# Hybrid decoder block, one core: the adaLN shift and later terms as VectorE dot products, the first scale on TensorE in pairs of tiles

## The chip, the core and the metric

One Trainium2 chip, one of its cores. TensorE multiplies matrices, VectorE and ScalarE work element by element on 128 partitions, GpSimd does little here, and DMA queues bring the weights from HBM. The metric is the device time of one launch in microseconds (us); the kernel before takes 1477.01 us, median of 3 runs (1475.06 to 1477.59).

## The reference

A decoder block on 256 tokens of width 2048, all in float32:

```
c_act = silu(c)
mod = c_act @ w_ada + b_ada                    # 2048 x 12288
sh1, sc1, gt1, sh2, sc2, gt2 = split(mod, 6)
h = rms_norm(x, g_pre_mix) * (1 + sc1) + sh1
z = h @ w_in                                   # 2048 x 8000
mix = (gate_a * mla(z) + gate_b * swa(z)) @ w_o
x = x + gt1 * rms_norm(mix, g_post_mix)
h = rms_norm(x, g_pre_ffn) * (1 + sc2) + sh2
u = causal_dwconv(h @ w_up)                    # 2048 x 11264
x = x + gt2 * rms_norm((silu(u1) * u2) @ w_down, g_post_ffn)
```

`mod` is a product of one row vector with a matrix of 100 MB: each of its weights is read once from HBM and used once. It makes 192 tiles of 128x1024 float32 (512 KB each), 32 for each of the six terms.

## The kernel before, in words

**Products.** Every large product is done three times over in a reduced float format: a weight tile `raw` is split into `whi` (ScalarE, L115) and `wlo` = raw - whi (VectorE, L116), the activations likewise (`split_pair`, L157 and L158), and TensorE adds hi·hi, hi·lo and lo·hi (`mm3`, L128 to L130, and its variants at L135 to L145).

**Order of work.** x comes in transposed (`xT`: channels on partitions). `early_z` multiplies h with half of `w_in` in six groups of k-tiles of 128 channels (`KGS` = 2, 2, 2, 2, 4, 4), called z0 to z5 below. While TensorE does group kg, a generator `early_gen` computes scale and shift of group kg + 1, scales xT with rstd, then with s1 and sh1 (L281, VectorE), and splits it to h. It is advanced by `pump`, once at each weight tile, at a rate. After the six groups come the attention (`step`, `late_z`, `pair_proj`), w_o, the passage to the second norm, w_up and w_down. The later four terms (gt1, s2, sh2, gt2) are generators `cols_gen`, pumped in z5, through the attention, w_o and w_up. The instructions of each engine are put in order ahead of time by a scheduler that simulates the engines; each engine then runs its own list in that order.

**How adaLN is computed.** `ada_gen` loads a tile of 1024 weights a partition (the contracted channels on partitions). On TensorE (L233) silu(c) is the stationary operand, as one column of a block of 32 (`cpad`), and the tile's columns are cut in four parts that go to the four groups of 32 columns of the array. On VectorE (L239, L241) the tile is multiplied with its silu(c) and added to `acc`; at the end four matmuls with `ones` (L246) add up the partitions. Either way the result lies in four rows, is copied to `rows` (L248) and turned into columns by matmuls with the identity (L269, L299). `SHARE` gives all tiles of groups 1 to 3 to TensorE, and every second tile of the last three to VectorE. The later terms are on VectorE alone.

**Buffers.** In the early groups adaLN tiles have four buffers of their own (`raw2`), w_in tiles five (`raw`); later all share the five. All loads are issued by one queue (SP, L94 and L101), in order.

Of the kernel before, what the change touches and what calls it, by code (L numbers as in the profile page):

```python
# [42 lines left out]
def block_kernel(ctx: ExitStack, tc: tile.TileContext, a, out: bass.AP):  # L43
    nc = tc.nc
    pe, act, dve, pool = nc.tensor, nc.scalar, nc.vector, nc.gpsimd
    PS = bass.MemoryType.PSUM
# [128 lines left out]
    xT = xp.tile([P, KC, T], F32, name="xT")  # L175
# [4 lines left out]
    ones = const.tile([P, P], F32, name="ones")  # L180
    pool.memset(ones, 1.0)
# [26 lines left out]
    for k in range(0, KC, 2):
        sq = xp.tile([P, 512], F32, tag="sq", bufs=2, name="sq").rearrange("p (a b) -> p a b", a=2)
        act.activation(sq, xT[:, k:k + 2, :], AF.Square)  # L210
        for i in range(2):
            pe.matmul(ps_ss[:, :T], ones, sq[:, i, :], start=(k + i == 0), stop=(k + i == KC - 1))
# [5 lines left out]
    def ada_gen(src, width, rows, col, on_pe, share=10**9, spread=False):  # L218


        nj = KC // src.shape[0]
        w = 4 * width
        n = src.shape[0]
        acc = None
        ps = bank(on_pe) if on_pe else None
        for t in range(n):
            raw = load_bg(src[t], nj * w, spread and t % 2 == 1)
            for i in range(nj):
                j = t * nj + i
                if on_pe and t % share != share - 1:  # L230
                    for g in range(4):
                        o = i * w + g * width
                        pe.matmul(ps[32 * g:32 * g + 32, :width], cpad[:, j, :], raw[:, o:o + width],  # L233
                                  start=(j == 0), stop=(j == KC - 1 and share > n))
                    continue
                r = raw[:, i * w:i * w + w]
                if acc is None:
                    acc = const.tile([P, WT], F32, tag="acc", bufs=1, name="acc")
                    dve.tensor_scalar(acc[:, :w], r, csil[:, j:j + 1], None, op0=ALU.mult)  # L239
                else:  # L240
                    dve.scalar_tensor_tensor(acc[:, :w], r, csil[:, j:j + 1], acc[:, :w], op0=ALU.mult, op1=ALU.add)  # L241
            yield
        if acc is not None:
            ps = ps if on_pe else bank("tp")
            for g in range(4):
                pe.matmul(ps[32 * g:32 * g + 32, :width], ones[:, :32], acc[:, g * width:g * width + width],  # L246
                          start=not on_pe, stop=True)
        act.copy(rows[:, col:col + width], ps[:, :width])  # L248

    rows = const.tile([P, 512], F32, name="rows")  # L250
# [4 lines left out]

    def early_gen(kg, k0, s):

        w = s * 64
# [9 lines left out]
        for b in range(nb):
            pe.matmul(ps[:, 4 * b:4 * b + 4], rows[:, b * P:(b + 1) * P], ident[:, 0:P:32], start=True, stop=True)  # L269

        pv = ps[:, :4 * nb].rearrange("p (b g) -> p g b", g=4)
        bs = bada[:, KC + k0:KC + k0 + s].rearrange("p (g b) -> p g b", g=2)
        s1v = s1[:, k0:k0 + s].rearrange("p (g b) -> p g b", g=2)
        dve.scalar_tensor_tensor(s1v, pv[:, 0:2, :], 1.0, bs, op0=ALU.add, op1=ALU.add)
        dve.tensor_tensor(s1[:, k0:k0 + s], s1[:, k0:k0 + s], gcol[:, G_MIX + k0:G_MIX + k0 + s], op=ALU.mult)
        dve.tensor_tensor(sh1[:, k0:k0 + s].rearrange("p (g b) -> p g b", g=2), pv[:, 2:4, :],
                          bada[:, k0:k0 + s].rearrange("p (g b) -> p g b", g=2), op=ALU.add)
# [11 lines left out]

    def cols_gen(which, dst, bofs, gofs):  # L290

        for half in range(2):
            yield from ada_gen(a["w_ada2"][which][half], T, rows, half * T, None)

        for _ in range(4 if which == 3 else 0):
            yield
        ps = bank("tp")
        for b in range(4):
            pe.matmul(ps[:, 4 * b:4 * b + 4], rows[:, b * P:(b + 1) * P], ident[:, 0:P:32], start=True, stop=True)  # L299

        dve.tensor_tensor(dst.rearrange("p (g b) -> p g b", b=4), ps[:, 0:16].rearrange("p (b g) -> p g b", g=4),
                          bada[:, bofs:bofs + KC].rearrange("p (g b) -> p g b", b=4), op=ALU.add)
# [212 lines left out]
    def step(h):  # L515
# [72 lines left out]
    warm = const.tile([P, 1], F32, name="warm")  # L588
# [242 lines left out]
    return w[:, cols].reshape(w.shape[0] // P, P, len(cols)).transpose(1, 0, 2)  # L831


def _layout(i):
# [8 lines left out]
    L["b_adaT"] = c_(ba.reshape(6 * KC, P).T)  # L843

    k0 = 0
    w1, wi = [], []
    win = i["w_in"].reshape(D, 8000)
    early = _early_cols()
    for s in KGS:
        sc = wa[:, D + k0 * P:D + (k0 + s) * P]  # L850
        sh = wa[:, k0 * P:(k0 + s) * P]
        m = np.concatenate([sc, sh], 1)
        nj = WT // (s * 256)
        w1.append(m.reshape(KC // nj, nj, P, s * 256).transpose(0, 2, 1, 3).reshape(KC // nj, P, WT))
# [13 lines left out]
    for n, j in enumerate((2, 3, 4, 5)):
        L[f"w_ada2_{n}"] = c_(wa[:, j * D:(j + 1) * D].reshape(KC, P, 4, 2, T).transpose(3, 0, 1, 2, 4).reshape(2, KC, P, WT))
# [44 lines left out]
```

## Time and profile before

| | |
|---|---|
| median of 3 runs | 1477.01 us (1475.06 to 1477.59) |
| the profiled execution | 1481.65 us, span 1479.9 us |
| TensorE (PE) busy | 1442.6 us, 97% |
| VectorE (DVE) busy | 1082.0 us, 73% |
| ScalarE (ACT) busy | 777.6 us, 53% |
| HBM | 351 MB read, 240 GB/s over the span |

The span is the part of the execution between the first and the last instruction; 1.75 us lie around it. Times below are counted from the start of the span. A float32 matmul is recorded as two records, so 8 instructions stand as x16. The end of a matmul is modelled, so the distance from one start to the next says more than its duration.

### The profile page before, as it was taken

The numbers are of one execution on the slowest core, as the hardware profiler recorded it, in microseconds if no ns is written. First come the engines' busy times: TensorE is split into PE (matmuls) and PEld (weight loads), VectorE is DVE, ScalarE is ACT, GpSimd is POOL, SyncE is SP. The second block draws the span as 40 slices with busy tenths as digits, with TensorE's granted clock in tenths as the row PEclk, the third lists the DMA queues.
The fourth block names the chain that finished last, engine by engine and source line by source line (L and its number), as shares of the span: only waits on it lengthen the run. The fifth ranks groups of instructions, "written<-read, shape, count | busy, mean of one in ns | idle before, by whom it ended". The sixth has DMA issues, their size and how long they took to land.

```text
span 1479.9 us, 24583 instructions
## 1 busy us (share of the span) xinstructions
PE 1442.6 (97%) x9506; PEld 1271.2 (86%) x9506; DVE 1082.0 (73%) x1558; ACT 777.6 (53%) x1242; POOL 56.9 (4%) x65
## 2 busy tenths in 40 slices
PE   7999999899999999999899999999999999999997
PEld 5988999899999999878788888888888888888886
DVE  3589968998887978868787788876776775444443
ACT  4522335465665746865655555755555554434342
POOL 0000000000000000000000101000000000000000
PEclk9999999999999999999999999999999999999999
DMA  9889958588787878579388788765555557555552
GB/s 373 304 313 369 339 178 259 162 273 302 255 301 250 293 243 291 180 268 371 130 278 264 245 262 267 235 206 188 190 190 189 187 189 250 186 198 188 195 190 97
DMA packets 101524, 356.96 MB, mean 241 GB/s; under 512 B 11760, under 2 KB 12208, under 8 KB 100896
## 3 DMA queue, kind: packets, MB, share of 16 engines
q1 hardware_dynamic: 99936, 350.82, 69.4%
q0 software_dynamic: 1472, 4.58, 1.2%
q8 instruction: 74, 1.21, 0.3%
q14 instruction: 42, 0.34, 0.1%
HBM read 351.11 MB, written 4.24 MB: 240 GB/s over the span
## 4 chain that ended last, share of the span: by engine, by line
PE 79%; DMA 10%; DVE 7%; issue 2%; ACT 2%; DVEq 0%; SPq 0%; ACTq 0%
PE bk_mm L135 11%; PE bk_sc L135 8%; PE bk_mm L128 7%; PE bk_mm L130 7%; PE bk_mm L129 7%; DMA raw<-in_w_ada_dram 6%; PE bk_mm L137 6%; PE bk_mm L143 4%; PE bk_mm L144 4%; PE bk_mm L145 4%; PE bk_sc L137 4%; PE bk_sc L143 3%; PE bk_sc L145 3%; PE bk_sc L144 3%; DVE acc L241 2%
## 5 line engine op out<-in xcount | busy, mean ns | idle before, releaser
L115 ACT CAST whi<-raw 128x1024 fp32r<-128x1024 f32 (+3 forms) x472 | 479.7, 1023 | 554.1 <-PE bk_mm L129 91.4
L116 DVE TENSOR_TENSOR wlo<-raw,whi 128x1024 fp32r<-128x1024 f32 (+3 forms) x472 | 567.7, 1209 | 275.2 <-ACT whi L115 272.5
L128 PE MATMUL bk_mm<-h,whi 128*128 128x256 f32 x976 | 282.6, 290 | 2.6 <-DVE pair L370 1.8
L130 PE MATMUL bk_mm<-h,wlo 128*128 128x256 f32 x976 | 277.7, 286 | 4.0 <-DVE wlo L116 4.0
L129 PE MATMUL bk_mm<-h,whi 128*128 128x256 f32 x976 | 278.0, 285 | 0.0
L135 PE MATMUL bk_mm<-h,whi 128*128 128x512 f32 x848 | 266.6, 396 | 0.8 <-ACT whi L115 0.8
L241 DVE SCALAR_TENSOR_TENSOR acc<-raw,csil,acc 128x1024 f32<-128x1024 f32 (+1 forms) x141 | 177.4, 1258 | 36.4 <-DMA raw<-in_w_ada_dram 35.7
L128 PEld LDWEIGHTS bk_mm<-h,whi 128*128 128x128 f32 x976 | 187.8, 193 | 15.8 <-issue 8.0
L137 PEld LDWEIGHTS bk_mm<-h,wlo 128*128 128x128 f32 x848 | 158.7, 188 | 42.0 <-DVE wlo L116 4.9
L130 PEld LDWEIGHTS bk_mm<-h,wlo 128*128 128x128 f32 x976 | 187.1, 192 | 6.5 <-DVE wlo L116 4.2
L129 PEld LDWEIGHTS bk_mm<-h,whi 128*128 128x128 f32 x976 | 188.0, 193 | 1.0 <-issue 1.0
L135 PE MATMUL bk_sc<-h,whi 128*128 128x512 f32 x560 | 176.2, 396 | 0.0
L137 PE MATMUL bk_mm<-h,wlo 128*128 128x256 f32 x848 | 167.3, 279 | 2.3 <-DVE wlo L116 2.2
L135 PEld LDWEIGHTS bk_mm<-h,whi 128*128 128x128 f32 x848 | 129.2, 189 | 1.6 <-ACT whi L115 1.0
L137 PEld LDWEIGHTS bk_sc<-h,wlo 128*128 128x128 f32 x560 | 104.9, 188 | 26.6 <-DVE wlo L116 2.1
L137 PE MATMUL bk_sc<-h,wlo 128*128 128x256 f32 x560 | 110.4, 279 | 0.9 <-DVE wlo L116 0.9
L135 PEld LDWEIGHTS bk_sc<-h,whi 128*128 128x128 f32 x560 | 85.3, 189 | 0.5 <-ACT sa L755 0.4
L370 DVE TENSOR_TENSOR pair<-pair,bk_mm 128x512 f32<-128x512 f32 (+1 forms) x100 | 65.6, 673 | 19.0 <-PE bk_mm L130 15.0
L143 PE MATMUL bk_sc<-whi,g 128*128 128x512 f32 x176 | 68.6, 390 | 0.0
L143 PE MATMUL bk_mm<-whi,g 128*128 128x512 f32 x176 | 68.6, 390 | 0.0
L144 PE MATMUL bk_mm<-wlo,g 128*128 128x512 f32 x176 | 68.5, 389 | 0.0
L145 PE MATMUL bk_mm<-whi,g 128*128 128x512 f32 x176 | 68.5, 389 | 0.0
(195 smaller groups left out, 2052.2 us busy)
## 6 DMA issues: line engine op xcount, KB each, us to landing
raw<-in_w_ada_dram SPq DMA_DIRECT2D x192, 512.0 KB, 5.1
raw<-in_w_up_dram SPq DMA_DIRECT2D x176, 512.0 KB, 4.7
raw<-in_w_in_dram SPq DMA_DIRECT2D x116, 512.0 KB, 5.4
raw<-in_w_down_dram SPq DMA_DIRECT2D x88, 512.0 KB, 4.6
raw<-in_w_o_dram SPq DMA_DIRECT2D x32, 512.0 KB, 5.9
raw<-in_w_uqn_dram SPq DMA_DIRECT2D x16, 384.0 KB, 4.1
bias<-trow POOLq DMA_DIRECT2D x16, 256.0 KB, 4.9
raw<-in_w_ukv_dram SPq DMA_DIRECT2D x16, 256.0 KB, 4.3
```

The lines of the kernel that those rows point to most:

```text
L115: act.copy(hi[:, :n], raw[:, :n])
L116: dve.tensor_tensor(lo[:, :n], raw[:, :n], hi[:, :n].bitcast(F32), op=ALU.subtract)
L128: pe.matmul(o, wh, xh, start=start, stop=False)
L129: pe.matmul(o, wh, xl, start=False, stop=False)
L130: pe.matmul(o, wl, xh, start=False, stop=stop)
L135: pe.matmul(o, w[0], x[2], start=start and i == 0, stop=False)
L137: pe.matmul(o[:, :T], w[1], x[0], start=False, stop=stop and i == 1)
L143: pe.matmul(o, ch, wh, start=start, stop=False)
L144: pe.matmul(o, ch, wl, start=False, stop=False)
L145: pe.matmul(o, cl, wh, start=False, stop=stop)
L241: dve.scalar_tensor_tensor(acc[:, :w], r, csil[:, j:j + 1], acc[:, :w], op0=ALU.mult, op1=ALU.add)
L370: dve.tensor_tensor(pairs[i][:, :wd], pairs[i][:, :wd], b[:, :wd], op=ALU.add)
```

## The change

Weights of adaLN are laid out anew on the host: those of the shift sh1 and of the four later terms with the output channels on partitions (`_dots`). A tile is then half of the inputs of 128 output channels, and one VectorE instruction (`dot`, tensor_tensor_reduce) multiplies it with `csb`, silu(c) on all partitions, and adds along the row; a second one for the other half starts from the first one's sum. What comes out is already a column: `acc`, L246, L248, L299 and L301 go for these terms. The scale s1 stays on TensorE for all six groups; its tiles now hold the scale alone, 32·s columns to each column group where there were 64·s. After the first group two tiles at a time are held and then multiplied, the second loaded first. `SHARE` goes. h's scaling with s1 and sh1 moves from VectorE to ScalarE. The squares of x are added up on VectorE, and two matmuls sum over partitions in place of 16. `csb` is made at the start by 16 transposes and 4 ScalarE copies. `ones` becomes a broadcast column, and `pT` has two buffers where it had three.

```
-                ht = xT[:, kk, :]
-                dve.tensor_scalar(ht, ht, s1[:, kk:kk + 1], sh1[:, kk:kk + 1], op0=ALU.mult, op1=ALU.add)
+                act.activation(ht, ht, AF.Identity, scale=s1[:, kk:kk + 1], bias=sh1[:, kk:kk + 1])
...
+    def dot(src, t, dst, cols, init, spread=False):
+        cc, kh = t // 2, t % 2
+        raw = load_bg(src[t], WT, spread)
+        to = half if kh == 0 else dst[:, cols + cc:cols + cc + 1]
+        dve.tensor_tensor_reduce(raw, raw, csb[:, kh * WT:kh * WT + WT], 1.0,
+                                 bada[:, init + cc:init + cc + 1] if kh == 0 else half,
+                                 op0=ALU.mult, op1=ALU.add, accum_out=to)
...
+        for t in range(2 * s):
+            held.append((t, load_bg(a["w_ada1s"][kg][t], WT)))
+            if kg == 0 or len(held) == 2:
+                start = t < 2 if kg else t == 0
+                for u, raw in reversed(held):
+                    for i in range(nj):
+                        for g in range(4):
+                            o = i * w + g * width
+                            pe.matmul(ps[32 * g:32 * g + 32, :width], cpad[:, u * nj + i, :], raw[:, o:o + width],
+                                      start=start and i == 0, stop=t == 2 * s - 1 and i == nj - 1 and u == held[0][0])
+                    start = False
+                held = []
+            yield
+            dot(a["w_ada1h"][kg], t, sh1, k0, k0, kg == 0)
+            yield
...
-            pT = at.tile([P, 384], F32, tag="pT", bufs=3, name="pT")
+            pT = at.tile([P, 384], F32, tag="pT", bufs=2, name="pT")
```

TensorE's list at the start, before: `L212` are the sums of squares, `L233` adaLN tiles of group 0.

```order
L212 MATMUL bk_tp<-sq,ones 128x256 x10
L233 MATMUL bk_sc<-raw_155,cpad 32x128 x8
L212 MATMUL bk_tp<-sq,ones 128x256 x4
L233 MATMUL bk_sc<-raw,cpad 32x128 x8
L212 MATMUL bk_tp<-sq,ones 128x256 x2
...
L269 MATMUL bk_tp<-c_ident,rows 128x4
L233 MATMUL bk_sc<-raw_255,cpad 32x128 x8
L128 MATMUL bk_mm<-h,whi 128x256 x3
```

The same place now: `L148` makes csb, `L224` is the sum of squares, `L267` the scale's tiles; `L127` is the first product with h.

```order
L148 MATMUL bk_mm<-c_ident,csil 128x128 x16
L267 MATMUL bk_sc<-raw_176,cpad 32x64 x16
L224 MATMUL bk_tp<-ssx,one 128x256 x2
L267 MATMUL bk_sc<-raw_197,cpad 32x64 x16
L267 MATMUL bk_sc<-raw_218,cpad 32x64 x16
L267 MATMUL bk_sc<-raw_239,cpad 32x64 x16
L278 MATMUL bk_tp<-c_ident,rows 64x2 x2
L127 MATMUL bk_mm<-h,whi 128x256 x3
```

Eight tiles of group 0 became four; no tile of group 1 stands any more ahead of the first product. Further on, in z1, two tiles of group 2 in TensorE's list before, with products of h around them:

```order
L233 MATMUL bk_sc<-raw_791,cpad 32x128 x2
L128 MATMUL bk_mm<-h,whi 128x256
...
L130 MATMUL bk_mm<-h,wlo 128x256
L233 MATMUL bk_sc<-raw_791,cpad 32x128 x6
L233 MATMUL bk_sc<-raw_807,cpad 32x128 x8
L128 MATMUL bk_mm<-h,whi 128x256
```

And two tiles of group 2 now, in the same stage:

```order
L267 MATMUL bk_sc<-raw_805,cpad 32x64
L127 MATMUL bk_mm<-h,whi 128x256
...
L267 MATMUL bk_sc<-raw_805,cpad 32x64 x4
L127 MATMUL bk_mm<-h,whi 128x256
...
L267 MATMUL bk_sc<-raw_805,cpad 32x64 x11
L267 MATMUL bk_sc<-raw_732,cpad 32x64 x6
L127 MATMUL bk_mm<-h,whi 128x256
...
L267 MATMUL bk_sc<-raw_732,cpad 32x64 x10
```

So a pair that is written as one run of 32 instructions is cut by the scheduler. In the whole list of groups 1 to 5 there are 31 such pieces (3 in z0, then 7, 8, 6 and 7).

ScalarE's list where the first h is made, before:

```order
L214 ACTIVATE rstd<-bk_tp,epst 128x256
L248 COPY rows<-bk_sc 128x128
L115 CAST whi<-raw 128x1024
L157 CAST h<-xT 128x2x256
L115 CAST whi<-raw 128x1024 x2
```

And now:

```order
L226 ACTIVATE rstd<-bk_tp,epst 128x256
L274 COPY rows<-bk_sc 128x64
L114 CAST whi<-raw 128x1024
L287 ACTIVATE xT<-xT,sh_167,s_166 128x256 x2
L156 CAST h<-xT 128x2x256
L114 CAST whi<-raw 128x1024 x2
```

The two scalings stand between the first split of a w_in tile and the split of h.

## Rows read from the trace of the kernel before

**Rows 1.** Windows: us, busy per engine (x instructions), granted clock, DMA share, GB/s
```profile
24.00:222.00 198.00, 196.50 (x1819) 177.51 (x1812) 153.19 (x211) 73.82 (x92) 0.00 (x0) 0.99 0.86 308
113.00:148.00 35.00, 34.47 (x303) 30.20 (x303) 34.27 (x48) 10.70 (x12) 0.00 (x0) 1.00 0.99 372
222.00:300.00 78.00, 72.10 (x568) 69.92 (x567) 68.47 (x88) 41.04 (x59) 2.55 (x5) 0.98 0.68 217
300.00:650.00 350.00, 346.61 (x2695) 322.21 (x2694) 298.67 (x567) 223.87 (x485) 17.29 (x28) 1.00 0.80 264
```
**Rows 2.** Timeline of TensorE around one adaLN tile: start, us, engine, line
```profile
31.94 0.28 PE L130 MATMUL bk_mm<-h,wlo 128*128 128x256 f32 x1
32.15 0.65 PE L233 MATMUL bk_sc<-raw,cpad 128*32 128x128 f32 x16
32.73 0.39 PE L128 MATMUL bk_mm<-h,whi 128*128 128x256 f32 x1
```
**Rows 3.** The same view, several tiles in a row at the start
```profile
16.41 1.96 PE L233 MATMUL bk_sc<-raw,cpad 128*32 128x128 f32 x64
```
**Rows 4.** Windows of L233 alone, z0 to z4: PE busy, PEld busy, clock, DMA
```profile
24.00:56.00 32.00, 6.10 (x128) 3.26 (x120) 0.91 0.98 372
56.00:90.00 34.00, 6.75 (x134) 3.80 (x134) 1.00 0.83 279
90.00:113.00 23.00, 4.24 (x74) 1.93 (x74) 1.00 0.89 321
113.00:148.00 35.00, 4.47 (x56) 1.10 (x56) 1.00 0.99 372
148.00:222.00 74.00, 5.09 (x56) 1.23 (x56) 1.00 0.74 258
```
**Rows 5.** Windows of L246 alone (sums over partitions)
```profile
24.00:222.00 198.00, 1.66 (x24) 0.68 (x24) 0.99 0.86 308
...
300.00:650.00 350.00, 3.19 (x40) 0.79 (x40) 1.00 0.80 264
...
730.00:1000.00 270.00, 1.28 (x16) 0.32 (x16) 1.00 0.74 244
```
**Rows 6.** Windows of L269 alone (turning into columns, early groups)
```profile
24.00:222.00 198.00, 2.16 (x14) 1.95 (x14) 0.99 0.86 308
```
**Rows 7.** Windows of L299 alone (turning into columns, later terms)
```profile
300.00:650.00 350.00, 2.22 (x16) 2.10 (x16) 1.00 0.80 264
...
730.00:1000.00 270.00, 0.95 (x8) 0.98 (x8) 1.00 0.74 244
```
**Rows 8.** Groups by form: xcount | busy us, mean ns | idle before, releasers
```profile
L241 DVE SCALAR_TENSOR_TENSOR acc<-raw,csil,acc 128x1024 f32<-128x1024 f32 x134 | 172.1, 1284 | 36.4 <-DMA raw<-in_w_ada_dram 35.7
...
L549 DVE CUSTOM_DVE_ANT_0 sm<-bk_sc,bias,c_sink 128x256 f32<-128x256 f32 x32 | 15.5, 483 | 0.0
...
L549 DVE CUSTOM_DVE_ANT_0 sm<-bk_sc,bias,c_sink 128x128 f32<-128x128 f32 x32 | 11.1, 346 | 0.4 <-PE bk_sc L544 0.3
...
L549 DVE DVE_READ_ACCUMULATOR2_ANT mx<- 128x1 f32 x96 | 8.3, 86 | 0.0
...
L750 ACT ACTIVATE u<-o,cw 128x256 f32<-128x256 f32 x88 | 52.8, 600 | 16.4 <-DVE o L748 16.3
```
**Rows 9.** Windows of L241 alone
```profile
300.00:650.00 350.00, 89.63 (x70) 1.00 0.80 264
```
**Rows 10.** Timeline at the start, all engines: the way to the first product
```profile
21.84 0.73 DVE L281 TENSOR_SCALAR xT<-xT,s,sh 128x256 f32<-128x256 f32 x2
22.37 1.05 ACT L115 CAST whi<-raw 128x1024 fp32r<-128x1024 f32 x1 [1.40 <-DMA raw<-in_w_in_dram]
23.32 0.61 ACT L157 CAST h<-xT 128x512 fp32r<-128x512 f32 x1
...
24.68 0.58 PE L128 MATMUL bk_mm<-h,whi 128*128 128x256 f32 x1
```
**Rows 11.** Waits of the DMA queue's engine: waited for, us, times, longest
```profile
SPq L101 <- PE bk_sc L233: 56.4, 35, 3.5
```

More of the change, by code (lines that the diff above doesn't have):

```diff
@@ L179, in block_kernel @@
     ident = const_load("ident", [P, P])
-    ones = const.tile([P, P], F32, name="ones")
-    pool.memset(ones, 1.0)
+    one = const.tile([P, 1], F32, name="one")
+    pool.memset(one, 1.0)
+    ones = one.broadcast_to([P, P])
     epst = const.tile([P, 1], F32, name="epst")
@@ L197, in block_kernel @@
     csil = const.tile([P, KC], F32, name="csil")
-    cth = const.tile([P, KC], F32, name="cth")
+    cth = xp.tile([P, KC], F32, name="cth")
     act.activation(cth, cT, AF.Tanh, scale=0.5)
@@ L204, in block_kernel @@
     dve.tensor_copy(cpad[:, :, 0:1], csil.rearrange("p (k o) -> p k o", o=1))
-    ps_ss = bank("tp")
[L208 to L212, printed above, removed]
+    warm = const.tile([P, 1], F32, name="warm")
+    act.activation(warm, epst, AF.Sqrt, scale=0.0, bias=epst)
+    csb = const.tile([P, D], F32, name="csb")
+    for k in range(0, KC, 4):
+        b = bank("mm")
+        for j in range(4):
+            turn_pe(b[:, j * P:j * P + P], csil[:, k + j:k + j + 1].broadcast_to([P, P]))
+        act.copy(csb[:, k * P:(k + 4) * P], b)
+    ssx = xp.tile([P, 512], F32, name="ssx")
+    for k in range(0, KC, 2):
+        sq = ssx if k == 0 else xp.tile([P, 512], F32, tag="sq", bufs=2, name="sq")
+        act.activation(sq.rearrange("p (a b) -> p a b", a=2), xT[:, k:k + 2, :], AF.Square)
+        if k:
+            dve.tensor_tensor(ssx, ssx, sq, op=ALU.add)
+    ps_ss = bank("tp")
+    for i in range(2):
+        pe.matmul(ps_ss[:, :T], ones, ssx[:, i * T:i * T + T], start=i == 0, stop=i == 1)
     rstd = xp.tile([P, T], F32, name="rstd")
@@ L215, in block_kernel @@
     dve.reciprocal(rstd, rstd)
[L218 to L250, printed above, removed]
+    def dot(src, t, dst, cols, init, spread=False):
[5 more added lines that the diff above has]
+                                 op0=ALU.mult, op1=ALU.add, accum_out=to)
+    half = const.tile([P, 1], F32, name="half")
+    rows = xp.tile([P, P], F32, name="rows")
     s1 = const.tile([P, KC], F32, name="s1")
@@ L256, in early_gen @@
     def early_gen(kg, k0, s):
-        w = s * 64
+        w, width = s * P, s * 32
+        nj = WT // w
         with ExitStack() as order:
@@ L263, in early_gen @@
                 dve.tensor_tensor(xT[:, k, :], xT[:, k, :], rstd, op=ALU.mult)
-        yield from ada_gen(a["w_ada1"][kg], w, rows, 0, "sc", SHARE[kg], kg == 0)
-        nb = w // P
-        ps = bank("tp")
[L268 to L277, printed above, removed]
+        ps = bank("sc")
+        held = []
[10 more added lines that the diff above has]
+                    start = False
+                held = []
+            yield
+            dot(a["w_ada1h"][kg], t, sh1, k0, k0, kg == 0)
+            yield
+        act.copy(rows[:, :width], ps[:, :width])
+        ps = bank("tp")
+        if s == 2:
+            for u in range(2):
+                pe.matmul(ps[64 * u:64 * u + 64, 0:2], rows[:, 0:64], ident[:, 32 * u:P:64], start=True, stop=True)
+        else:
+            pe.matmul(ps[:, 0:4], rows, ident[:, 0:P:32], start=True, stop=True)
+        s1v = s1[:, k0:k0 + s]
+        dve.scalar_tensor_tensor(s1v, ps[:, 0:s], 1.0, bada[:, KC + k0:KC + k0 + s], op0=ALU.add, op1=ALU.add)
+        dve.tensor_tensor(s1v, s1v, gcol[:, G_MIX + k0:G_MIX + k0 + s], op=ALU.mult)
         for k in range(k0, k0 + s, 2):
@@ L290, in cols_gen @@
     def cols_gen(which, dst, bofs, gofs):
-        for half in range(2):
-            yield from ada_gen(a["w_ada2"][which][half], T, rows, half * T, None)
-        for _ in range(4 if which == 3 else 0):
+        for t in range(2 * KC):
+            dot(a["w_ada2"][which], t, dst, 0, bofs)
             yield
[L297 to L302, printed above, removed]
         if dst is s2:
@@ L586, in step @@
         dve.tensor_tensor(mixs[h // 2][:, e * T:e * T + T], tm[:, 0:T], tm[:, T:512], op=ALU.add)
-    warm = const.tile([P, 1], F32, name="warm")
     bg["gen"] = [cols_gen(0, gt1, 2 * KC, G_PMIX), cols_gen(2, s2, 4 * KC, G_FFN), cols_gen(1, sh2, 3 * KC, None)]
@@ L831, in _blocks, with _dots @@
     return w[:, cols].reshape(w.shape[0] // P, P, len(cols)).transpose(1, 0, 2)
+def _dots(w):
+    return w.T.reshape(w.shape[1] // P, P, 2, WT).transpose(0, 2, 1, 3).reshape(-1, P, WT)
 def _layout(i):
@@ L845, in _layout @@
     k0 = 0
-    w1, wi = [], []
+    w1, w1h, wi = [], [], []
     win = i["w_in"].reshape(D, 8000)
@@ L849, in _layout @@
     for s in KGS:
[L850 to L854, printed above, removed]
+        nj = WT // (s * P)
+        m = wa[:, D + k0 * P:D + (k0 + s) * P]
+        w1.append(m.reshape(KC // nj, nj, P, s * P).transpose(0, 2, 1, 3).reshape(KC // nj, P, WT))
+        w1h.append(_dots(wa[:, k0 * P:(k0 + s) * P]))
         m = win[k0 * P:(k0 + s) * P][:, early]
@@ L863, in _layout @@
     for g in range(len(KGS)):
-        L[f"w_ada1_{g}"] = c_(w1[g])
+        L[f"w_ada1s_{g}"] = c_(w1[g])
+        L[f"w_ada1h_{g}"] = c_(w1h[g])
         L[f"w_in1_{g}"] = c_(wi[g])
@@ L868, in _layout @@
     for n, j in enumerate((2, 3, 4, 5)):
[L869 removed]
+        L[f"w_ada2_{n}"] = c_(_dots(wa[:, j * D:(j + 1) * D]))
     L["gcol"] = c_(np.concatenate([i[n].reshape(-1, P).T for n in
@@ L906 @@
         a[name] = nc.dram_tensor(f"in_{name}_dram", v.shape, mybir.dt.from_np(v.dtype), kind="ExternalInput").ap()
-    for base, n in (("w_ada1", len(KGS)), ("w_in1", len(KGS)), ("w_ada2", 4)):
+    for base, n in (("w_ada1s", len(KGS)), ("w_ada1h", len(KGS)), ("w_in1", len(KGS)), ("w_ada2", 4)):
         a[base] = [a[f"{base}_{g}"] for g in range(n)]
```

1 line of the change is left out of this document (removed).

## The prediction

> **What bounds the kernel now.** I read the windows by stage first, then the timeline around one adaLN tile, then the groups by form, the waits and the start. From 24 to 222 us TensorE is busy 196.5 of 198 us, from 300 to 650 us 346.6 of 350 [rows 1]. Busy can flatter there, since ends are modelled; but the timeline shows products of h starting one behind the other without a hole, so what is taken off TensorE's list in these stages is time, as long as nothing else stands as close behind. Two things do, in places. In z0 (24 to 56 us) and z3 (113 to 148 us) the DMA engines are at 0.98 and 0.99 and move 372 GB/s [rows 4], and the bytes do not change. In z3 VectorE, too, is busy 34.3 of 35 us [rows 1]. From 222 to 300 us TensorE does wait, 5.9 us of 78, while VectorE is busy 68.5; no adaLN work of TensorE stands there. So TensorE's saving counts in z1, z2, z4 and after 300 us, and is doubtful in z0 and z3.
>
> **Term 1, TensorE in the early groups.** Before, one tile delays the products by a piece: the start of the matmul after it comes 0.58 us behind its own start, and it is recorded as 0.65 us of busy [rows 2], so I take busy as cost. Several tiles in a row give the inner price: 64 records take 1.96 us, 16 take 0.65, so a step of four records (one for each column group) takes (1.96 - 0.65) / 12 = 0.109 us, and a piece has 0.65 - 4 x 0.109 = 0.21 us of its own [rows 2, 3]. From 24 to 222 us adaLN costs 26.65 us for L233, 1.66 for L246 and 2.16 for L269 [rows 4 to 6].
>
> After, groups 1 to 3 have 12 tiles of 8 steps with 64 columns each, groups 4 and 5 have 16 tiles of 4 steps with 128 columns: 96 + 64 steps, in 31 pieces by the new order. No row shows a step of 64 columns. From above it costs as much as one of 128 columns, 0.109 us, if the four weight loads set the pace; from below half, 0.055 us, if the columns do. I take 0.109, since that row is the nearest and the step still has four loads and four matmuls. Then z0 to z4 cost 4.1, 5.0, 5.2, 4.7 and 4.9 us (32 steps and 3, 7, 8, 6 and 7 pieces each): 23.9 in place of 26.65, and L246 falls away; L278 and L280 cost about what L269 did. Of this I count z1 (-1.8), z2 (+1.0), z4 (-0.2), two thirds of L246 (-1.1) and half of z0's 2.0: **-3 us**. The ends: 0, if the DMA queue takes it all, and -10 with half-price steps (96 x 0.054 = 5.2 more).
>
> [...] No row of this trace decides it, as 128 columns fit both readings.
>
> **Term 2, TensorE in the later terms.** L246 and L299 go altogether. From 300 to 650 us they cost 3.19 + 2.22 = 5.4 us, from 730 to 1000 us 1.28 + 0.95 = 2.2 us [rows 5, 7]. The rest lies between 650 and 730 us, where TensorE waits for the norm anyhow; I count it as nothing. Of the 7.6 I take **-7 us**, because TensorE is idle 3.4 us of the 350 and some of the gaps will only be shifted. The ends are 0 and -8.
>
> **Term 3, VectorE.** The instruction of a dot product is in the trace with one operand in PSUM: 346 ns for 128 elements, 483 for 256, so 1.07 ns for an element, and 483 + 768 x 1.07 = 1305 ns for 1024; its readout adds 86 ns at most [rows 8]. L241, which reads two SBUF operands of 1024, takes 1284 ns [rows 8]. So a dot costs 1.28 to 1.39 us; I take 1.30. There are 160, 209 us in all, against at least 172 before (the 134 of full size alone). Off VectorE go h's scalings, 0.73 us for two [rows 10], 5.8 for 16. The net is at most +31 us over 900, and VectorE has 45 us free from 24 to 222 and 51 from 300 to 650 [rows 1]. In z3, where it has none, it gets 8 dots for 8 accumulations (+0.2 to +0.9 us) and loses four scalings (-1.6). Cost: **0**, at most +2 if the readout counts in z3 and from 222 to 300 us.
>
> **Term 4, the start.** Before, the first product begins at 24.68 us, the scalings at 21.84, and h is split from 23.32 on, after the first split of a weight tile at 22.37 [rows 10]. Now the two scalings stand on ScalarE behind that split, which waits for its DMA; with scale and bias from SBUF such an instruction takes about 600 ns (L750 in [rows 8]). So: 23.42, then 1.2 us, then 0.61: h at 25.2 in place of 23.9. Against that, a tile of group 1 no longer stands ahead of the first product on TensorE, and the sums of squares need 2 matmuls in place of 16 there. I take **+1 us**. From below -1, if the sums end that much sooner; from above +3, if the now emptier TensorE stays longer at its lower clock: z0 ran at 0.91 granted, z1 at 1.00 [rows 4].
>
> **Term 5, the rest.** h's scalings of the later groups lie on ScalarE, which is busy 74 of 198 us [rows 1]; four of them and a wait behind a split are 2 to 3 us, while TensorE still has the end of the group before to do. `pT` with two buffers makes ScalarE wait at most where a step follows closely on the one before; I take 0 for both, with +2 as the upper end.
>
> **Sum.** -3 - 7 + 0 + 1 + 0 = -9 us on the profiled execution: 1481.65 to 1472.65. That execution lies 4.64 us above the median of the runs, so the median comes to **1468 us**. With this mechanism alone it lies between 1459 and 1475.
>
> **Rivals.**
> *The saving is real in full.* Steps at half price, nothing lost to DMA: -10 - 8 - 0 = -18, 1459 us. For it speaks that TensorE is idle only 1.5 us from 24 to 222 us [rows 1]; against it, 372 GB/s in two of five stages. Chance 0.13.
>
> *Hidden anyway.* z0 to z4 go by the DMA queue, and from 300 us on by the loop of load, split and release of the five buffers (DMA 0.80, VectorE 0.85 busy [rows 1]). Then only 0 to 3 us are left: 1474 to 1478 us. Against it: the nearly unbroken chain of products. Chance 0.18.
>
> *Slower: a dot with both operands in SBUF runs at half rate.* Each of its operands is 32 bits wide and it must keep a sum as well; the dots in the trace had one operand in PSUM. Each would then take 1.07 x 1024 = 1.09 us more. In z3 8 dots are +8.7 against 1.6 saved: +7. From 300 to 650 us some 75 tiles (70 L241 [rows 9] and the first ones of the sums) make +82 against 51 us free: +31. It decides as soon as the dots there take over 51 / 75 = 0.7 us more each. From 222 to 300 us about +2. Together +40 - 9: 1508 us. Against it: L241 reads two such operands at 1.25 ns an element [rows 8]. [...] L241's full rate shows that two sources alone do not do it; for one with an accumulator no row is there. Chance 0.07.
>
> *Slower: pairs starve the loads.* A held tile keeps one of four buffers until the next lands, and SP, which issues all loads in order, waited 56.4 us in 35 places for TensorE to release such a buffer already [rows 11]. With 14 pairs in groups 1 to 5 and about 1 us lost at each in stages at the DMA's limit: +14 - 9, 1482 us; it decides from 0.7 us a pair. Against it: half the tiles now are released by VectorE, at once. Chance 0.08.
>
> **How the numbers follow.** Forecast 0.54, then 0.13, 0.18, 0.07 and 0.08. Within 0.2% (3 us, about what a measurement of this kernel can tell) falls most of the hidden case and a little of the forecast: 0.17. Slower: the two last ones and a small part from the start and the shifted orders: 0.16. Faster: 0.67. The range 1457 to 1484 leaves out the half-rate case and some of the tails.
>
> **What would show it.** Dots of 1.28 to 1.39 us confirm term 3, over 2 us the half-rate case. L267 from 24 to 222 us at about 24 us of busy confirms the step price, under 20 the other reading. z1 ends earlier by 2 us and z3 keeps its 35 us at 372 GB/s, if I have the limits right; the stretch from 300 us to the end of the attention should shrink by about 5 us. The first product at 25 to 26 us confirms term 4. TensorE idle in the early stages for DMA would mean the pairs starve the loads, and a VectorE over 95% from 300 to 650 us that I sized the dots too small.

## The result, and the profile after

The changed kernel takes 1465.37 us (median of 4, 1464.50 to 1467.70) against 1477.30 (median of 4, 1475.06 to 1478.21): a ratio of 0.9916, 95% interval 0.9904 to 0.9929, or 12 us less. The forecast was 1468.0. The sign was right and the sum near; terms of it were mis-sized, in opposite directions. The profiled execution lies at 1465.97 us (span 1464.1), that of before 4.35 us above its median. Lines of the changed kernel are those of its own profile: L267 is the scale's matmul (L233 before), L236 the dot product, L287 h's scaling (L281 before), L127 to L129 the products with h (L128 to L130 before), L93 and L100 the loads (L94 and L101 before).

Windows of the changed kernel: us, busy time of PE, PEld, DVE, ACT, POOL (x instructions), granted clock, DMA share, GB/s. 107 to 144 us is z3 here, 212 to 300 lies in z5 (compare [rows 1]). The windows called z0 to z4, here as in the prediction, are those in which TensorE's list holds adaLN of groups 1 to 5; the products with h end later, those of z3 from 129.5 to 164.8 us (134.8 to 170.4 before):

```profile
24.00:222.00 198.00, 194.40 (x2037) 184.68 (x2038) 163.95 (x232) 84.28 (x111) 0.00 (x0) 0.98 0.88 313
107.00:144.00 37.00, 36.46 (x382) 34.05 (x381) 34.96 (x54) 12.32 (x15) 0.00 (x0) 1.00 0.97 355
212.00:300.00 88.00, 83.61 (x679) 81.83 (x679) 80.84 (x118) 49.39 (x73) 2.55 (x5) 1.00 0.71 231
300.00:650.00 350.00, 344.46 (x2615) 319.98 (x2614) 299.87 (x634) 224.06 (x478) 16.27 (x28) 1.00 0.80 264
```

TensorE is still busy nearly all the time, and VectorE stays at 86% from 300 to 650 us, in spite of the dots. So what came off TensorE's list is what there can be to gain. L267 alone in z0 to z4, PE and PEld busy, clock, DMA share, GB/s (compare [rows 4]):

```profile
24.00:52.00 28.00, 2.49 (x128) 2.01 (x128) 0.89 1.01 390
52.00:84.00 32.00, 3.49 (x128) 2.36 (x128) 1.00 0.87 299
84.00:107.00 23.00, 3.79 (x128) 2.49 (x128) 1.00 0.94 317
107.00:144.00 37.00, 5.12 (x128) 3.51 (x128) 1.00 0.97 355
144.00:212.00 68.00, 5.33 (x128) 3.45 (x128) 1.00 0.79 278
```

That is 20.2 us where the prediction had 23.9. L278 and L280, which turn the row into columns, add 0.85 and 0.56 us from 24 to 222 us (compare [rows 6]):

```profile
24.00:222.00 198.00, 0.85 (x12) 0.59 (x12) 0.98 0.88 313
...
24.00:222.00 198.00, 0.56 (x4) 0.61 (x4) 0.98 0.88 313
```

So adaLN costs TensorE 21.6 us there, against 26.65 + 1.66 + 2.16 = 30.5 before [rows 4 to 6], where `SHARE` gave it all tiles of groups 0 to 2, counted from 0 as elsewhere here: 8.8 us less, and the 9 us or so of [rows 5, 7] and of the w_o stage are gone altogether. The dot products, by form (xcount | busy us, mean ns of one | idle before):

```profile
L236 DVE CUSTOM_DVE_ANT_0 raw<-raw,csb,c_b_adaT 128x1024 f32<-128x1024 f32 x80 | 103.5, 1294 | 23.8 <-DMA raw<-in_w_ada_dram 21.7 <-issue 1.1 <-DMA raw<-in_w_ada1s_dram 0.6
L236 DVE CUSTOM_DVE_ANT_0 raw<-raw,csb,half 128x1024 f32<-128x1024 f32 x80 | 102.5, 1281 | 29.7 <-DMA raw<-in_w_ada_dram 28.6 <-DMA raw<-in_w_ada1h_dram 0.8
L236 DVE DVE_READ_ACCUMULATOR2_ANT half<- 128x1 f32 x80 | 6.7, 84 | 0.0
```

They stand at 1281 to 1294 ns, with 84 ns for the readout, as L241 did [rows 8]; from 300 to 650 us dots and readouts together take 96.68 us, 7 more than L241 did [rows 9]:

```profile
300.00:650.00 350.00, 96.68 (x150) 1.00 0.80 264
```

The start, all engines (compare [rows 10]):

```profile
21.89 0.15 DVE L282 SCALAR_TENSOR_TENSOR s<-bk_tp,c_b_adaT 128x2 f32<-128x2 f32 x1
...
22.38 1.05 ACT L114 CAST whi<-raw 128x1024 fp32r<-128x1024 f32 x1 [2.84 <-DMA raw<-in_w_in_dram]
23.33 1.09 ACT L287 ACTIVATE xT<-xT,sh,s 128x256 f32<-128x256 f32 x2
24.45 0.62 ACT L156 CAST h<-xT 128x512 fp32r<-128x512 f32 x1
...
25.13 1.01 PE L127 MATMUL bk_mm<-h,whi 128*128 128x256 f32 x3 [5.26 <-ACT h L156]
```

s1 is ready at 22.2, but ScalarE first splits a weight tile that came late, and then scales; the first product waits 5.26 us in all and starts at 25.13. The wait of the load queue for TensorE, 56.4 us in 35 places before [rows 11], is now:

```profile
SPq L100 <- PE bk_sc L267: 24.2, 17, 3.3
```

**Where the time went.** Both kernels run the same 8754 records of products and transposes outside adaLN. Counting their columns gives a measure of progress, and the time at equal progress shows where one execution is ahead. In the table 0 is a second profile of the kernel before (`b_again` below); negative is earlier, in us; the times in the first column are those of `b_again`. `a_again` is a second profile of the kernel after.

```
at     before   after  a_again  x_early  x_early_dve0  x_late  b_pt2  a_dve0  a_dvescale  a_pt3  c_both
  26    +0.0    +0.8    +0.8    +0.4      -0.5         +1.7   -0.6    -0.3     -0.3      +0.7    -0.4
  56    +1.2    -1.3    -1.4    -0.9      -2.8         +4.3   +2.2    -2.6     -1.8      -0.7    -2.0
 113    +1.2    -5.4    -5.4    -5.0      -8.4         +4.2   +2.2    -8.1     -7.4      -4.8    -7.6
 148    +1.2    -5.5    -5.5    -5.1      -9.5         +4.2   +2.2    -7.5     -8.1      -4.8    -8.3
 217    +1.2    -4.6    -4.6    -4.2      -8.5         +4.2   +2.2    -6.5     -7.0      -3.5    -6.6
 300    +3.2    -5.8    -4.5    -3.3      -9.1         +4.9   +2.0    -6.9     -6.6      -4.6    -5.5
 660    +1.7    -9.6   -11.1    -2.5      -7.9         -3.0   +2.7   -14.3    -12.0     -14.1   -13.1
1000    +3.4   -12.3   -12.6     0.0      -7.6         -6.0   +2.3   -14.8    -14.8     -17.4   -16.7
```

Two executions of the kernel before differ by up to 3.4 us along the way, so one entry is good to some 3 us. The profile of `x_early` is its slowest run, 5.4 us above its median, so its column is of little use behind 217 us. After gains 6 us from the first product to 113 us (z0 to z2), nothing more in z3 and z4, and 7.7 us from 217 to 1000 us (8.0 in `a_again`).

The order of the lists helps to place an edit. Two profiles of one kernel show the same instructions of TensorE, VectorE and ScalarE in the same order. `after`, `a_dve0` and `a_dvescale` have one order behind 230 us, `a_pt3` and `c_both` another, different from about 335 us on; `b_pt2` has that of before up to 340 us.

### The profile page after: what moved, and what is told of

Same layout as the page of the kernel before. It is cut to its first block, busy times and chain, and to the rows that moved or that the text cites. A ratio compares the mean times of both kernels' runs of the same rounds, so it can differ in the third digit from the quotient of the medians.

```text
span 1464.1 us, 24829 instructions
## 1 busy us (share of the span) xinstructions
PE 1418.5 (97%) x9570; PEld 1263.0 (86%) x9570; DVE 1099.8 (75%) x1707; ACT 785.6 (54%) x1255; POOL 58.8 (4%) x65
## 4 chain that ended last, share of the span: by engine, by line
PE 62%; DMA 10%; DVE 5%; issue 3%; ACT 2%; DVEq 0%; ACTq 0%
PE bk_mm L134 8%; DMA raw<-in_w_ada_dram 8%; PE bk_sc L134 5%; PE bk_mm L127 4%; PE bk_mm L129 4%; PE bk_mm L128 4%; PE bk_mm L144 4%; PE bk_mm L143 4%; PE bk_mm L142 4%; PE bk_mm L136 4%; PE bk_sc L142 3%; PE bk_sc L144 3%; PE bk_sc L143 3%; PE bk_sc L136 3%; PE bk_o L578 2%
## 5 line engine op out<-in xcount | busy, mean ns | idle before, releaser
L127 PE MATMUL bk_mm<-h,whi 128*128 128x256 f32 x976 | 282.3, 290 | 11.5 <-ACT h L156 5.3
L129 PE MATMUL bk_mm<-h,wlo 128*128 128x256 f32 x976 | 277.8, 285 | 1.5 <-DVE wlo L115 1.4
L128 PE MATMUL bk_mm<-h,whi 128*128 128x256 f32 x976 | 277.6, 285 | 0.0
L127 PEld LDWEIGHTS bk_mm<-h,whi 128*128 128x128 f32 x976 | 187.3, 192 | 19.7 <-DVE pair L368 6.3
L129 PEld LDWEIGHTS bk_mm<-h,wlo 128*128 128x128 f32 x976 | 187.0, 192 | 4.0 <-issue 2.0
L128 PEld LDWEIGHTS bk_mm<-h,whi 128*128 128x128 f32 x976 | 187.4, 192 | 0.6 <-issue 0.6
L236 DVE CUSTOM_DVE_ANT_0 raw<-raw,csb,half 128x1024 f32<-128x1024 f32 x80 | 102.5, 1281 | 29.7 <-DMA raw<-in_w_ada_dram 28.6
L236 DVE CUSTOM_DVE_ANT_0 raw<-raw,csb,c_b_adaT 128x1024 f32<-128x1024 f32 x80 | 103.5, 1294 | 23.8 <-DMA raw<-in_w_ada_dram 21.7
L142 PE MATMUL bk_mm<-whi,g 128*128 128x512 f32 x176 | 68.6, 390 | 0.0
```

What stands on the lines that cost most here:

```text
L127: pe.matmul(o, wh, xh, start=start, stop=False)
L128: pe.matmul(o, wh, xl, start=False, stop=False)
L129: pe.matmul(o, wl, xh, start=False, stop=stop)
L142: pe.matmul(o, ch, wh, start=start, stop=False)
L236: dve.tensor_tensor_reduce(raw, raw, csb[:, kh * WT:kh * WT + WT], 1.0, bada[:, init + cc:init + cc + 1] if kh == 0 else half, op0=ALU.mul ...
```

## The experiments

Ratios are against the kernel before, run beside each, with 95% intervals; us are such a ratio times its median (1478 to 1480).

**A second profile of before** (`b_again`, no edit).

> The kernel before, unchanged, for a second profile. By progress of the products common to both kernels (8754 records, matched by the columns done), the kernel after stands 6.5 us ahead at 113 us, 5.8 at 250, 9.1 at 300, 11.3 at 700, 10.5 at 800 and 15.7 at 1000. The profile of before lies 4.4 us above its median, so 3 to 5 of these should not be the change's. If those 4 us are an accident of one execution between 830 and 930 us, this profile shows the gap against after at 1000 us at 11 to 12 and TensorE without the 2.7 us of idle in 830 to 880; if they belong to the kernel, it shows 15 again.

Measured: span 1476.5. At 1000 us after is 12.3 ahead of it, not 15.7. TensorE in 830 to 880 us, first here, then in the profile of before:

```profile
830.00:880.00 50.00, 49.88 (x290) 42.60 (x289) 39.85 (x51) 23.73 (x36) 4.23 (x2) 1.00 0.74 243
```

```profile
830.00:880.00 50.00, 47.28 (x271) 39.51 (x270) 38.69 (x49) 25.81 (x38) 4.24 (x2) 1.00 0.77 253
```

The 2.7 us of idle were one execution's. A comparison of the first two traces alone would have credited 15.7 us to the change.

**The early part alone** (`x_early`): after, with the later terms and pT of before, and some small tiles placed elsewhere for room.

```diff
+        for half in range(2):
+            yield from ada_gen(a["w_ada2"][which][half], T, rows, half * T, None)
-            dot(a["w_ada2"][which], t, dst, 0, bofs)
+            pT = at.tile([P, 384], F32, tag="pT", bufs=3, name="pT")
```

> The early part alone (scale on TensorE by pairs, first shift by dots, squares added on VectorE, h's scaling on ScalarE), the four later terms as in the kernel before (L241's way, with the four ones matmuls and rows at their end), pT with three buffers. Theory now: a step of 64 columns costs about half a step of 128, so the early part is worth 6 to 7 us: 1470 to 1471. The prediction as it stood: 3 gained and 1 lost, 1475. Rival (what shows early is only order, and is lost in z3 and z5): no change, 1477.

Measured: 0.9965 (0.9952 to 0.9978), 5.2 us less (3.3 to 7.1). Neither the prediction's 2 nor quite the 6 to 7.

**The later terms alone** (`x_late`): before, with csb, dot and their layout from after, and

```diff
-            yield from ada_gen(a["w_ada2"][which][half], T, rows, half * T, None)
+            dot(a["w_ada2"][which], t, dst, 0, bofs)
+            pT = at.tile([P, 384], F32, tag="pT", bufs=2, name="pT")
```

> The four later terms alone as dot products, the early groups as before (scale and shift on TensorE, L241's way for every second tile of the last three groups), csb added at the start, pT with two buffers. The prediction as it stood: 7 us gained, 1470, 5 of them between 300 and 650 us. Theory now: 4 to 6 gained, 1471 to 1473, most of it before 300 us and between 730 and 1000 us, with 2 to 3 between 300 and 650. Rival (hidden by the loop of load, split and release): 0 to 2, 1475 to 1477.

Measured: 0.9953 (0.9939 to 0.9967), 7.0 us less (4.9 to 9.0): the prediction's 7, and 5.2 + 7.0 make up the 12 of the whole. By the table it loses 3 to 4 us ahead of 56 us, where csb now stands in front of the old early part and the first product starts at 26.14 us (24.68 before), and gains 7.9 from 300 to 660 us and 3.0 after that. The theory's place for it (most before 300 us and after 730) was wrong.

**Two pT buffers in the kernel before** (`b_pt2`).

```diff
-            pT = at.tile([P, 384], F32, tag="pT", bufs=3, name="pT")
+            pT = at.tile([P, 384], F32, tag="pT", bufs=2, name="pT")
```

> The kernel before with two pT buffers in place of three, nothing else. The prediction: no cost, 1477 within 2 us. Rival: the second and third transpose of a step wait for products with pT, and the 300 to 650 us get longer by some 0.2 us in each of 16 steps, 3 us: 1480; then the later terms' saving of 5 us there was eaten by this.

Measured: 1.0012 (1.0000 to 1.0023), 1.8 us more (0 to 3.4); on its own at the edge of what can be told. Its profile does not place that cost in the attention: it is 2.2 us late at 56 us already, before any pT, and gains or loses no more than 0.7 us from there to 660 us. TensorE's waits for pT from 300 to 650 us are 1.6 us here, and with three buffers, in before, as long:

```profile
PE bk_o L575 <- ACT pT L571: 1.7, 2, 0.9
```

**The price of a step** (`a_quad`; the scale of groups 1 to 3 comes out four times too large).

```diff
+                        n = 4 if kg in (1, 2, 3) else 1
+                        for q in range(n):
                             for g in range(4):
```

> The kernel after, with every step of 64 columns of groups 1 to 3 issued four times (so their scale comes out four times too large): 96 steps more by three, 288, all in z0 to z2. If the four weight loads set the pace, as the prediction took it (0.109 us), z0 to z2 get 31 us longer and the run takes 1497. If the columns set it (0.055 us, as 32 records in 0.65 us in after say), 16 us longer and 1481. Less than 16 would say that the steps partly lie in holes of TensorE there, as in z0 at the DMA's limit.

Measured: 1497.39 us, 32 more than after: by the time alone, the price that the prediction took. The trace says otherwise. A long piece without a hole, of the TensorE timeline:

```profile
81.65 2.66 PE L269 MATMUL bk_sc<-raw,cpad 128*32 128x64 f32 x176
```

and in after the same view at a short one, 64 columns, then 128:

```profile
46.48 0.28 PE L129 MATMUL bk_mm<-h,wlo 128*128 128x256 f32 x1
46.69 1.10 PE L267 MATMUL bk_sc<-raw,cpad 128*32 128x64 f32 x64
47.72 0.39 PE L127 MATMUL bk_mm<-h,whi 128*128 128x256 f32 x1
...
109.22 1.08 PE L267 MATMUL bk_sc<-raw,cpad 128*32 128x128 f32 x32
```

112 more records cost 2.66 - 1.10 = 1.56 us, 0.056 for four: half of the 0.109 at 128 columns [rows 2, 3]. (Four records are two matmuls, half of the four column groups; the prediction calls them a step all the same, and its sums count them alike before and after.) And 64 records of 64 columns take as long as 32 of 128. So the 1152 added records are worth 16 us, and the rest is something else. The waits of TensorE in this run from 24 to 222 us (us in total, times, longest) name it in part:

```profile
PE bk_sc L269 <- issue: 5.8, 4, 2.0
PE bk_mm L127 <- ACT h L156: 4.9, 1, 4.9
PE bk_mm L127 <- issue: 2.0, 1, 2.0
```

"issue" is time in which TensorE waited for nothing that the profile shows, 7.8 us of it. Each of the four runs of 204 to 244 records has one such hole inside, of 1 to 2 us, after 137 to 164 records; a fifth stands among products behind the first of these runs, and the runs of 160 and 176 have none. The timeline shows one run with its hole:

```profile
34.48 2.14 PE L269 MATMUL bk_sc<-raw,cpad 128*32 128x64 f32 x137
37.78 1.75 PE L269 MATMUL bk_sc<-raw,cpad 128*32 128x64 f32 x107 [1.16 <-issue]
```

Behind the fifth, 2.0 us long, products start 0.21 us apart for a while in place of 0.12; from 24 to 52 us the granted clock was 0.82 here, 0.89 in after. What fills the holes isn't shown, and with the clock some 8 of the 32 us are not sized. The run's time fits the wrong theory by accident.

**No pairs** (`a_single`).

```diff
-            if kg == 0 or len(held) == 2:
+            if True:
-                start = t < 2 if kg else t == 0
+                start = t == 0
```

> The kernel after with each scale tile multiplied as it lands, none held: 47 pieces between products of h in place of 33. Theory: a piece costs 0.21 us of its own, so 3 us more, 1468. Rival (pairs starve the loads): holding a tile costs more than its piece, and without pairs it gets faster by 2 to 5 us, 1460 to 1463, with z0 and z3 shorter.

Measured: 1465.68 us, 0.9924 (0.9907 to 0.9941); after has 0.9916. TensorE's adaLN took 25.1 us from 24 to 222 us where after took 21.8 (from the start of the product ahead of each piece to the start of the one behind it, less 0.12 us), 3.3 more as expected; the time rose by about 1, and the intervals allow both 0 and 3. By the traces 2.3 us came back: TensorE's waits for pair adds in this stretch, explained below, are 2.3 us in after and none here. The queue waited longer for TensorE, not less, though with more and single holds:

```profile
SPq L100 <- PE bk_sc L267: 33.7, 21, 3.2
```

So pairs don't starve the loads.

**h's scaling back on VectorE** (`a_dve0`, group 0 alone, as shown; `a_dvescale`, the VectorE line for all groups).

```diff
-                act.activation(ht, ht, AF.Identity, scale=s1[:, kk:kk + 1], bias=sh1[:, kk:kk + 1])
+                if kg == 0:
+                    dve.tensor_scalar(ht, ht, s1[:, kk:kk + 1], sh1[:, kk:kk + 1], op0=ALU.mult, op1=ALU.add)
+                else:
+                    act.activation(ht, ht, AF.Identity, scale=s1[:, kk:kk + 1], bias=sh1[:, kk:kk + 1])
```

> The kernel after with h's scaling by s1 and sh1 back on VectorE. Theory of the prediction's terms 4 and 5: the first product comes about 1 us sooner (VectorE does two in 0.73 us without the split in front), the later groups do not care except z3, where VectorE is full: 1464 to 1466. Rival: the scaling stands behind dots on VectorE in all groups, h of each next group is late, and it costs 1 us a group, 1470.

> The kernel after with h's scaling on VectorE in group 0 alone, ScalarE in groups 1 to 5 as in after. Of the 4.7 us that VectorE's scaling gave back in all groups, term 4 put 1 at the start. Theory: 1 to 1.5 us come from group 0 (first product near 24.1 us in place of 25.1), the rest from the other groups: 1464. Rival: the whole loss sits in the start and the lower clock behind it: 1461.

Measured: 1460.66 us, 0.9882 (0.9861 to 0.9903), and 1462.42 us, 0.9893 (0.9878 to 0.9909). By the runs the scaling on ScalarE costs some 5 us, and group 0 alone gives back some 3.5 of them. The start in `a_dve0`, all engines:

```profile
22.37 0.73 DVE L288 TENSOR_SCALAR xT<-xT,s,sh 128x256 f32<-128x256 f32 x2
22.43 1.04 ACT L114 CAST whi<-raw 128x1024 fp32r<-128x1024 f32 x1 [2.54 <-DMA raw<-in_w_in_dram]
23.38 0.61 ACT L156 CAST h<-xT 128x512 fp32r<-128x512 f32 x1
24.03 0.69 DVE L157 TENSOR_TENSOR h<-xT,h 128x512 fp32r<-128x512 f32 x1 [0.92 <-ACT h L156]
24.05 1.01 PE L127 MATMUL bk_mm<-h,whi 128*128 128x256 f32 x3 [3.73 <-ACT h L156]
```

VectorE scales beside the split, and the first product comes 1.08 us sooner. This repeats: 25.13, 25.19, 25.11 and 24.75 us in `after`, `a_again`, `a_pt3` and `x_early`, 24.05, 24.06, 23.93 and 23.92 in `a_dve0`, `a_dvescale`, `c_both` and `x_early_dve0`. A second place repeats as well. Late in z3's products, a dot and a split stand ahead of a pair add (the addition of finished products from their PSUM bank) on VectorE, and TensorE waits for the bank, 1.8 to 2.1 us in the first four of these profiles and in none of the last four. In after:

```profile
154.51 1.29 DVE L236 CUSTOM_DVE_ANT_0 raw<-raw,csb,half 128x1024 f32<-128x1024 f32 x1
...
155.71 1.23 DVE L115 TENSOR_TENSOR wlo<-raw,whi 128x1024 fp32r<-128x1024 f32 x1
156.85 1.89 DVE L368 TENSOR_TENSOR pair<-pair,bk_mm 128x512 f32<-128x512 f32 x3
...
157.60 0.39 PE L127 MATMUL bk_mm<-h,whi 128*128 128x256 f32 x1 [1.80 <-DVE pair L368]
```

From 24 to 222 us TensorE's waits for pair adds come to 2.3 us in `after` and `a_again`, 1.6 in `a_dve0` (the longest 0.6) and 0.3 and 0.2 in `a_dvescale`. As `a_single` scales on ScalarE and has none of them, the wait goes with the order of VectorE's list and not with the scaling as such. So for `a_dve0` the start and these waits make 1.8 us; the table has 1.9 at 217 us (-6.5 against -4.6), and 2.4 for `a_dvescale`. Behind 230 us the lists are those of after, so what the profiles differ by there is one execution against another (`after` and `a_again`: 1.5 us at 660), and the traces show about 2 of the 3.5 to 5 us. Whether the groups after the first care at all, the two runs don't tell.

**Three pT buffers in after** (`a_pt3`).

```diff
-            r = at.tile([P, 512], F32, tag=tag, name=tag)
+            r = at.tile([P, 512], F32, tag=tag, name=tag, bufs=1 if tag == "ropeq" else 2)
-            pT = at.tile([P, 384], F32, tag="pT", bufs=2, name="pT")
+            pT = at.tile([P, 384], F32, tag="pT", bufs=3, name="pT")
```

> The kernel after with three pT buffers again; room for it from ropeq, which gets one buffer instead of two (used at every second pair only). Theory: before with two pT took 0.12% longer (1.8 us), so this gives 1 to 3 us between 300 and 650 us: 1463. Rival: pT cost nothing, and the one ropeq buffer makes the second half of the pairs wait: 1465 to 1468.

Measured: 1461.73 us, 0.9897 (0.9880 to 0.9913). The waits of TensorE from 300 to 650 us, after first, with all that it lists, then `a_pt3`:

```profile
PE bk_mm L142 <- ACT whi L114: 1.6, 1, 1.6
PE bk_mm L127 <- ACT whi L114: 1.4, 1, 1.4
PE bk_sc L542 <- DVE mx L547: 1.1, 1, 1.1
PE bk_o L573 <- ACT pT L569: 1.0, 1, 1.0
PE bk_o L578 <- ACT pT L569: 0.4, 1, 0.4
```

```profile
PE bk_mm L127 <- ACT whi L114: 1.4, 1, 1.4
PE bk_mm L142 <- ACT whi L114: 1.0, 1, 1.0
```

The 1.4 us for pT are gone, and the 1.1 us for mx with them. But that is not the third buffer's doing: `a_again`, with two buffers and the list of after, has neither wait either,

```profile
PE bk_mm L127 <- ACT whi L114: 1.4, 1, 1.4
PE bk_mm L142 <- ACT whi L114: 1.2, 1, 1.2
PE bk_tp L148 <- ACT sm L561: 0.5, 1, 0.5
```

and `c_both`, with three buffers, waits for pT:

```profile
PE bk_o L578 <- ACT pT L569: 0.5, 1, 0.5
PE bk_o L573 <- ACT pT L569: 0.3, 1, 0.3
```

The gain of 3 to 4 us is in the runs (all four lie below all nine of `after` and `a_again`), and in the table it stands behind 300 us, where the list is another. Whether the buffer, `ropeq` or the new order makes it isn't shown.

**Both together** (`c_both`: the edits of `a_dvescale` and `a_pt3`).

> The kernel after with h's scaling on VectorE and three pT buffers (ropeq with one): both runs before were faster than after, by 4.7 and 3.6 us of median. Theory (term 5 of the prediction was wrong: these two edits of the change each cost time, in different stages, and the saving of TensorE is in full): the two add up, 1457 to 1459. Rival (one of them, or both, are a matter of the scheduler's order and of noise of 2 us): no better than the better of the two, 1460 to 1463.

Measured: 1460.92 us, 0.9884 (0.9871 to 0.9898). It falls in the rival's range: 17 us below before (15.1 to 19.1) and no better than `a_dvescale`. In the table the scaling gives it 3.1 us on `a_pt3` at 217 us, as in the other pairs; behind that, with one and the same list, `c_both` gains 10.1 us and `a_pt3` 13.9, so executions differ by as much as is to be explained. Whether the two add in part isn't settled.

**After again** (`a_again`, no edit).

> The kernel after, unchanged, beside the others on one chip, and with a second profile. 1465 within 2 us. If a_dvescale and a_pt3 gained by their edits, this stays at 1464 to 1467; if they gained by the chip of their runs, it comes out near 1461.

Measured: 1466.11 us, 0.9918 (0.9906 to 0.9931), so after stands where it stood, and the gains of the others are not the chip's.

**The early part with group 0 scaled on VectorE** (`x_early_dve0`: `x_early` with the edit of `a_dve0`).

> The early part alone, as in x_early, with h's scaling of group 0 on VectorE. Counted from start to start, adaLN takes 30.4 us of TensorE from 24 to 222 us in the kernel before and 21.8 in after, 8.6 less; x_early gained 5.1. Theory: the rest was lost at the start, where ScalarE's scaling makes h late, as a_dve0 gained 3.7 on after; so this gives 8 to 9 us on before, 1469 to 1470, and the first product comes 1 us sooner than in x_early. Rival (DMA in z0 and z3 takes what the list gains, and a_dve0 gained by its order in the attention): 5 to 6, 1472 to 1473.

Measured: 1470.01 us, 0.9933 (0.9914 to 0.9951), 9.9 less (7.3 to 12.7), where `x_early` has 5.2. The first product comes at 23.92 (24.75 in `x_early`), the waits for pair adds fall from 2.3 to 0.5 us, and at 217 us it is 8.5 us ahead: with these two delays gone, the early part gives back about all that it takes off TensorE.

## Why the prediction came out right, and where it was wrong

**What bounds it: right.** TensorE's list sets most of the time. The 8.8 us less early and some 9 less in the later terms make 18; `x_early_dve0` and `x_late` alone gain 9.9 and 7.0, and `c_both` 17.

**Term 1: the mechanism right, the size wrong.** I took 0.109 us for four records of 64 columns, the upper end, on the ground that the nearest row still had four loads and four matmuls. It is 0.056, half of what 128 columns took: the columns set the pace. So adaLN fell by 8.8 us on TensorE and not by 4.4, and the 3 that I counted should have been 7 to 9. The limit in z0 was there (3.6 us off L233 and L267, 2.1 gained from 26 to 56 us, where I counted 1). The one in z3 was not tested: L267 takes 5.12 us there and L233 took 4.47 [rows 4], so the list had next to nothing to give. I had named half-price steps as the lower end (-10) and gone by the nearest row, which could not decide.

**Term 2: right, in part by luck.** -7 against -7.0 (4.9 to 9.0) in `x_late`; but by its profile that is the net of a start 3 to 4 us late and a gain of about 11 behind 300 us, where some 9 came off the list. Its place, mostly 300 to 650 us, was right: 7.9 us from 300 to 660 in `x_late`, 3.8 in after and 6.6 in `a_again`.

**Term 3: right.** 1281 to 1294 ns and 84 for the readout; VectorE is at 86% from 300 to 650 us. The half-rate rival is refuted: no run shows its 1.09 us more, as L241, with two float32 operands in SBUF, took 1284 ns [rows 8], and the dot, which also keeps a sum, 1281 to 1294. (Four scalings are 4 x 0.365 = 1.5 us, not the 1.6 of this term; nothing hangs on it.)

**Term 4: the start itself right, its price not.** The first product came at 25.13, within 25 to 26: 0.45 us later than before, and 1.08 later than in `a_dve0`, where +1 was forecast. But the runs say 3.7 us (`a_dve0`) and 4.7 (`x_early_dve0`) for that one edit, and the table 1.9 and 4.3 ahead of 217 us. The upper end of +3 took an emptier TensorE to stay longer at a lower clock, which the runs don't settle: ahead of 24 us the granted clock was 0.98 before (170 records) and 0.84 in after (152), but 1.00 in `a_dve0` (152 as well). I stopped at the first product. A wait for a pair add 130 us later, 1.8 us, comes with the order that VectorE's list then has, and I did not follow the lists that far.

**Term 5: too small, cause open.** I put 0. For the scaling of the later groups the runs leave 1.8 us (`a_dvescale` against `a_dve0`), with intervals that overlap. Three pT buffers with one `ropeq` buffer gain 3 to 4 us on after, more than the +2 that I gave as the end; two pT buffers on before cost 1.8 us by the runs (0 to 3.4) and nothing that its profile can place. The waits for pT do not follow the number of buffers, so my mechanism, ScalarE waiting for a buffer, is neither shown nor refuted as the price.

So the forecast came out near because errors nearly cancelled, and that is luck: a saving sized 8 us too small (some 18 and not 10) and costs sized some 4 us too small (`c_both` takes 4.5 to 5.2 us less than after and `a_again`, where the sum had +1). With the right price of a step alone, and nothing of it lost to DMA, the sum would have been -8.8 - 7 + 1 = -14.8, 1462 us.

**The rivals.** "Real in full" had the right saving on TensorE (18 us, by steps at half price) and missed the costs. "Hidden anyway" and "pairs starve the loads" fell: the queue waits 24.2 us for TensorE in place of 56.4.

**Open.** What makes the gain of `a_pt3`, the buffer, `ropeq` or the order; whether the two repairs add; what the holes of "issue" are.

## What to carry to other kernels

Where TensorE is full, count its list from start to start and expect it back, but price the small edits that come with a change (an operation moved to another engine ahead of the first product, a buffer given up for room) one by one: here they ate some 5 of 17 us. When two readings of a price lie a factor of two apart, measure the step that has half the columns, in place of taking the nearest row. Look at the trace of an experiment whose time fits: it may fit for another reason. And before a wait that is gone is called the gain of an edit, take a second profile of the unedited kernel: here it had lost the same wait.

## What the runs showed of the hardware that was not expected

- A dot product of 1024 with both operands in SBUF and an accumulator takes 1281 to 1294 ns and 84 for its readout; L241, without an accumulator, took 1284 [rows 8].
- Four matmuls, one in each of the four column groups (eight records), cost by their columns: 0.11 us at 64 columns (176 records against 64), 0.22 at 128 (64 against 16 [rows 2, 3]).
- Long runs of such short matmuls had holes that no shown wait explains: four in `a_quad`, 5.8 us in all and the longest 2.0, one in each run of 204 to 244 records, none in those of 160 and 176.
- The granted clock at the start differed between executions of one kernel. From 24 to 30 us (columns as in the windows above), the profile of before, then `b_again`:

```profile
24.00:30.00 6.00, 6.00 (x51) 4.96 (x44) 4.83 (x6) 2.10 (x2) 0.00 (x0) 0.52 1.02 408
```

```profile
24.00:30.00 6.00, 6.00 (x61) 5.26 (x54) 4.86 (x6) 2.72 (x4) 0.00 (x0) 0.75 1.02 409
```

The same instructions in the same order, and over these 6 us TensorE was granted 0.52 in one and 0.75 in the other; at 56 us the two stand 1.2 us apart. A difference of a microsecond ahead of 30 us is no finding from a single profile.
